# One ring of weight tiles over three phases, and an FFN down projection taken by blocks of tokens

## The chip, the cores and the metric

The kernel runs on one core of a Trainium2 chip. The metric is the device time of one execution in microseconds (us). Engines are called as the profile calls them: PE (matmuls), PEld (the weight loads that go with them), DVE, ACT and POOL (elementwise work), SP (it issues most DMAs). PE's clock is granted at one of two levels, 2.4 GHz (1.00 in the profile) or 1.2 GHz (0.50).

## The reference, cut to what matters

512 tokens of width 1024 pass through two blocks. The first has a projection into attention, a state-space branch and gates, a cross attention over 256 memory tokens, and PEER, a layer of 16384 single-neuron experts. The second has a mixer of two linear-attention kinds and a convolutional FFN:

```python
h = h + merged @ w_out                       # phase 0
h = h + memory_cross_attention(...)          # phase 0
h = h + peer_ffn(rmsnorm(h), ...)            # phase 1: u = u_tab[e]; v = v_tab[e]
x = rmsnorm(h, norm_final)
x = x + rms_norm(hybrid_mixer(rms_norm(x)), norm_mix_post)                        # phase 2
x = x + rms_norm(conv_ffn(rms_norm(x)), norm_ffn_post)                            # phase 2
def conv_ffn(hn):
    g = dwconv3(hn @ w_gate)                 # 1024 -> 2816 = 22 tiles of 128
    return (gelu(g) * (hn @ w_up)) @ w_down  # 2816 -> 1024
```

## The kernel before

**Weights.** Every product is made from three matmuls: each operand is split into a high part and a low remainder, and high x high, high x low and low x high are added in PSUM. `wtile` (L161) does this for a weight tile of 128 x 1024: SP loads `raw` (L170), ACT writes `whi` (L172), DVE or POOL subtracts to get `wlo` (L175). Each of the three has a ring of buffers. The rings belong to a pool `wp` that `phase` (L1751) opens anew in each of three phases: 3, 2 and 2 buffers in phases 0 and 2, and 5, 4 and 4 in phase 1 (`WB`). A new pool lies on memory that the phase before has used, so its tiles wait until the last reader of that memory is done.

**Order.** The order on each engine is fixed when the program is built, from the order of the code and an estimate of when operands are there. An engine doesn't overtake at run time.

**Phase 0** ends with the output projection of the cross attention (8 weight tiles `w_co`), each of which adds into `h` (L872). **Phase 1**, `peer`: `peer_query` splits the normed activations (`fsh` on ACT, L245, `fsl` on DVE, L246), squares them for the norm (L263, L267) and runs 16 projections with `w_pq`. Then come 64 steps of `dense_u` (L1051, UONLY = 64), the U stage: the 384 tokens of three blocks against 128 experts each, 24 matmuls of 384 columns, and a gelu on ACT (L1057) into `al`, which four steps share and which is spilled to DRAM (`ad`, L1059), 768 KB at a time. Among these steps `peer_route` finds the experts, `gate_chunk` (L994) builds 12 chunks of dense gates, ACT copying them (L1014) into the staging tiles `stg` (two buffers of the tag, two tiles per chunk) and SP writing them out (L1017), and from step 32 on 24 gathers for the first token block: POOL's indirect DMAs into the ring `gr` of six buffers (L1022) and a DVE product (L1034). The V stage then runs 64 more `dense_u` and 128 `dense_v` with the spilled values read back.

**Phase 2** begins with `block2` (L1213): splits `bh`, `bl`; one projection (B2P = 1), `rms_pair` (L1180: 16 squares, sums on DVE and POOL at L1193, 16 matmuls at L1196 that sum over partitions, a chain of small steps that gives `rt`), `rbcast` (`rB`), then `proj_small` (48 columns for gates and low-rank inputs), three more projections, and `gates2` (L1353), a chain over ACT and DVE that gives `la` and `cum`. Four projections with a convolution follow (`mqk`, L1269 on), and a stepwise interleaving of `gla`, `mlstm` and three token-major projections `tm(0)` to `tm(2)`, whose matmuls fill PE between the others' steps. Four PSUM banks have the tag "mm", four "sm".

**FFN** (L1708): for three groups of `m` (8, 8 and 6 tiles of the 22), the gate and up projections of each `m`, its convolution, gelu and product, then the down projection of that group: for each of the 8 output tiles, 24 (18) matmuls with a weight tile of `w_fd` standing in PE and 512 tokens moving. Sums go to `ff` in SBUF, feature-major like the residual `x` (in `hx`). After the last tile the norm runs over the features, which lie on partitions: squares, sums, `rms_end` (L270), `rbcast` (L282), and `postnorm` (L1666) with two elementwise operations per tile of 128 x 512 on DVE and POOL, and eight output DMAs.

## Time and profile before

| | us |
|---|---|
| median of 3 runs (2997.66 to 2999.61) | 2999.13 |
| the profiled execution, its own time | 2997.53 |
| its span, first to last instruction | 2995.4 |
| PE busy | 2854.2 (95%), 14033 matmuls |
| DVE, ACT, POOL busy | 2138.7, 1276.9, 765.6 |

The profiled execution is 1.6 us below the median. Its span is 2.1 us shorter than its time. The mean granted clock of PE is 0.979. The rows on which the prediction rests stand behind the diff. "Releaser" is the instruction that ended an idle time. The start of an instruction is in us from the start of the span.

### The profile page before, as it was taken

Reading aid. Unit: us, or ns where it says so; the run is one execution under the profiler, and the core shown is the slowest. Engines: PE = TensorE matmul, PEld = TensorE weight load, DVE = VectorE, ACT = ScalarE, POOL = GpSimd, SP = SyncE. Lnnn points to the kernel's source line nnn. Section 1 sums busy time; section 2 is a strip of 40 time slices with the busy share of each in tenths; the row PEclk is TensorE's granted clock in tenths of the full one; section 3 lists DMA queues with packets and bytes.
Section 4 is the critical chain, followed back from the end, with each engine's and each line's share of the span. In section 5 each row is a group of like instructions: output and inputs, shape, how many; then the busy total and the mean of one; then the engine's idle time right before and its main releaser. Section 6 shows DMA issues by size and latency. Waiting matters only on the chain. (4 is left out here: it accounts for less than half of the span.)

```text
span 2995.4 us, 37951 instructions
## 1 busy us (share of the span) xinstructions
PE 2854.2 (95%) x14033; PEld 2415.6 (81%) x14033; DVE 2138.7 (71%) x3766; ACT 1276.9 (43%) x2159; POOL 765.6 (26%) x529
## 2 busy tenths in 40 slices
PE   7899999999998999989999999999988899799997
PEld 6767788888886899889988888888866677688886
DVE  7987865454557999986677777787875765564656
ACT  4356754332534347776333333333334343332222
POOL 3421320001201010111244444444533551310102
PEclk9999999999999999999999999999998899899998
DMA  4211112324412256778799899999932112233332
GB/s 134 78 53 47 64 57 96 100 85 141 141 57 91 93 197 201 232 240 263 271 332 339 327 345 327 339 329 336 345 147 70 57 43 64 63 99 98 98 93 70
DMA packets 177865, 491.36 MB, mean 164 GB/s; under 512 B 14833, under 2 KB 66289, under 8 KB 177489
## 3 DMA queue, kind: packets, MB, share of 16 engines
q1 hardware_dynamic: 140336, 353.42, 34.7%
q0 software_dynamic: 37344, 135.54, 12.9%
q8 instruction: 110, 1.80, 0.2%
q14 instruction: 75, 0.61, 0.1%
HBM read 445.84 MB, written 41.94 MB: 163 GB/s over the span
## 5 line engine op out<-in xcount | busy, mean ns | idle before, releaser
L172 ACT ACTIVATE whi<-raw 128x1024 fp32r<-128x1024 f32 (+2 forms) x508 | 535.1, 1055 | 1156.4 <-PE mm L187 446.4
L175 DVE TENSOR_TENSOR wlo<-raw,whi 128x1024 fp32r<-128x1024 f32 (+1 forms) x470 | 606.2, 1292 | 346.1 <-ACT whi L172 340.9
L186 PE MATMUL u<-nsh,whi 128*128 128x384 f32 x1024 | 346.2, 338 | 2.7 <-ACT al L1057 2.7
L1022 POOL DMA_INDIRECT gr<-u_tab,pidx x128 | 184.0, 1437 | 641.1 <-DVE gr L1034 490.8
L188 PE MATMUL u<-nsh,wlo 128*128 128x384 f32 x1024 | 345.0, 337 | 0.2 <-DVE wlo L175 0.2
L187 PE MATMUL u<-nsl,whi 128*128 128x384 f32 x1024 | 344.8, 337 | 0.0
L1022 POOL DMA_INDIRECT gr<-v_tab,pidx x128 | 199.9, 1562 | 214.0 <-DVE acc L1047 182.1
L1087 PE MATMUL acc<-whi,Wh 128*128 128x512 f32 x768 | 237.7, 391 | 0.0
L1089 PE MATMUL acc<-whi,Wl 128*128 128x512 f32 x768 | 237.0, 390 | 0.0
L186 PEld LDWEIGHTS u<-nsh,whi 128*128 128x128 f32 x1024 | 192.6, 188 | 5.3 <-ACT al L1057 3.0
L1093 PE MATMUL acc<-wlo,Wh 128*128 128x512 f32 x768 | 194.9, 389 | 0.0
L187 PEld LDWEIGHTS u<-nsl,whi 128*128 128x128 f32 x1024 | 192.7, 188 | 2.3
L188 PEld LDWEIGHTS u<-nsh,wlo 128*128 128x128 f32 x1024 | 192.3, 188 | 0.5 <-DVE wlo L175 0.5
L186 PE MATMUL mm<-ah,whi 128*128 128x512 f32 x424 | 173.1, 408 | 12.5 <-ACT whi L172 12.5
L188 PE MATMUL mm<-ah,wlo 128*128 128x512 f32 x424 | 170.0, 401 | 1.2 <-DVE wlo L175 1.2
L187 PE MATMUL mm<-al,whi 128*128 128x512 f32 x424 | 170.2, 401 | 0.0
L1089 PEld LDWEIGHTS acc<-whi,Wl 128*128 128x128 f32 x768 | 144.1, 188 | 31.4
L1093 PEld LDWEIGHTS acc<-wlo,Wh 128*128 128x128 f32 x768 | 144.1, 188 | 30.0
L1047 DVE SCALAR_TENSOR_TENSOR acc<-gr,act,acc 128x1024 f32<-128x1024 f32 x127 | 163.4, 1287 | 1.5
L1087 PEld LDWEIGHTS acc<-whi,Wh 128*128 128x128 f32 x768 | 143.3, 188 | 26.3
L1034 DVE SCALAR_TENSOR_TENSOR gr<-gr,xt 128x1024 f32<-128x1024 f32 x128 | 153.1, 1221 | 0.0
L186 PE MATMUL mm<-fh,whi 128*128 128x512 f32 x352 | 138.8, 396 | 7.2 <-ACT fh L245 7.2
(596 smaller groups left out, 6311.1 us busy)
## 6 DMA issues: line engine op xcount, KB each, us to landing
raw<-uT SPq DMA_DIRECT2D x128, 512.0 KB, 5.6
raw<-v_tab SPq DMA_DIRECT2D x128, 512.0 KB, 6.5
raw<-w_cm SPq DMA_DIRECT2D x61, 512.0 KB, 3.5
gd<-stg SPq DMA_DIRECT2D x24, 1024.0 KB, 8.4
Gl<-gd SPq DMA_DIRECT2D x32, 768.0 KB, 8.9
ad<-al SPq DMA_DIRECT2D x16, 768.0 KB, 5.7
al<-ad SPq DMA_DIRECT2D x16, 768.0 KB, 7.8
raw<-w_fg SPq DMA_DIRECT2D x22, 512.0 KB, 3.5
```

What stands on the lines that cost most here:

```text
L172: nc.scalar.activation(hi[:, :n], raw[:, :n], AF.Copy)
L175: self.paced = (eng or nc.vector).tensor_tensor(lo[:, :n], raw[:, :n], hi[:, :n].bitcast(F), op=OP.subtract)
L186: mm(ps, w[0][:, cs[k]], xh, start=k0 + k == ends[0], stop=False)
L187: mm(ps, w[0][:, cs[k]], xl, start=False, stop=False)
L188: mm(ps, w[1][:, cs[k]], xh, start=False, stop=k0 + k == k1)
L1022: self.nc.gpsimd.indirect_dma_start(out=t, out_offset=None, in_=self.I[tab], in_offset=bass.IndirectOffsetOnAxis(ap=self.idx[:, j:j + 1], ...
L1034: nc.vector.scalar_tensor_tensor(u, u, 1.0, self.xt, op0=OP.mult, op1=OP.mult, accum_out=self.act0[:, i:i + 1])
L1047: nc.vector.scalar_tensor_tensor(self.acc0, v, w, self.acc0, op0=OP.mult, op1=OP.add)
L1087: mm(self.accp[tt * 2 + hf], wh[:, ts], hi[:, cs[hf]], start=first, stop=False)
L1089: mm(self.accp[tt * 2 + hf], wl[:, ts], hi[:, cs[hf]], start=False, stop=False)
L1093: mm(self.accp[tt * 2 + hf], wh[:, ts], lo[:, cs[hf]], start=False, stop=last)
```

## The change

- `wp` is opened once, outside the phases, with rings of 3, 2 and 2; phase 1 gets a second pool `wpx` with 2, 2 and 2, and tiles take turns between the two, so the depths in each phase stay as they were.
- `gate_chunk` has four staging buffers in place of two.
- In the U stage the gelu writes into `al2`, a tile of two steps, taken from the ring `gr` that the gathers use, and is spilled in pairs (384 KB).
- `block2` starts with `proj_small` and three projections (B2P = 3) before `rms_pair`; `gates2` moves ahead of the evacuation of the projections; `tm(0)` runs as a whole before the `mqk` loop.
- The down projection turns round: `w_fd` is taken in rows, 22 tiles of 128 x 1024; the activations `gs` stand in PE and the weights move; eight PSUM banks collect 4 token blocks x 2 halves. The last `m` of a group (in the last group the last three, whose weights have slab tiles of their own, `own=True`) runs token block by token block. `x` is turned into token-major `xt` by 32 transposes in the first four `m`, `ff` lies in the memory of `hx`, the gain is a row `gB`, and the norm is a sum along the free axis (`accum_out` of the square). The output is written as rows of tokens, in halves.

```diff
@@ -96 +96 @@
     o["w_fu"] = _cm(a["ffn_w_up_2"][0])
-    o["w_fd"] = _cm(a["ffn_w_down_2"][0])
+    o["w_fd"] = a["ffn_w_down_2"][0]
+    o["frow"] = a["norm_ffn_post_2"]
     g = {
@@ -161 +162 @@
 
-    def wtile(self, src, n, eng=None):
+    def wtile(self, src, n, eng=None, own=False):
         nc = self.nc
...
             eng = nc.gpsimd
-        br, bh, bl = WB[self.ph]
-        raw = self.wp.tile([128, 1024], F, name="raw", tag="raw", bufs=br)
+        pick = lambda n, m: self.wpx if self.ph == 1 and self.wi % m >= n else self.wp
+        raw = pick(3, 5).tile([128, 1024], F, name="raw", tag="raw", bufs=pick(3, 5) is self.wp and 3 or 2)
         nc.sync.dma_start(raw[:, :n], src)
-        hi = self.wp.tile([128, 1024], R, name="whi", tag="whi", bufs=bh)
+        if own:
+            s = self.sl("wown", R)
+            hi, lo = s[:, 0:1024], s[:, 1024:2048]
+            nc.scalar.activation(hi, raw, AF.Copy)
+            nc.vector.tensor_tensor(lo, raw, hi.bitcast(F), op=OP.subtract)
+            return hi, lo
+        hi = pick(2, 4).tile([128, 1024], R, name="whi", tag="whi", bufs=2)
         nc.scalar.activation(hi[:, :n], raw[:, :n], AF.Copy)
-        lo = self.wp.tile([128, 1024], R, name="wlo", tag="wlo", bufs=bl)
+        lo = pick(2, 4).tile([128, 1024], R, name="wlo", tag="wlo", bufs=2)
         self.wi += 1
@@ -228 +235 @@
             mm(ps[0:n, :], lo[:, c], acts(k)[0], start=False, stop=k == 7)
-        return self.small_tm(ps, 0, n)
+        return ps
 
@@ -993 +1000 @@
         nc = self.nc
-        stg = [self.mid.tile([128, 2048], F, name="stg", tag="stg", bufs=2) for i in range(2)]
+        stg = [self.mid.tile([128, 2048], F, name="stg", tag="stg", bufs=4) for i in range(2)]
         for q in range(8):
@@ -1051 +1058 @@
         self.mms(ps[:, :384], (hi, lo), self.ns, 0, 8, 8)
+        if a < UONLY:
+            if a % 2 == 0:
+                self.al2 = self.gp.tile([128, 1024], F, name="al2", tag="gr")[:, 0:768].rearrange("p (a t) -> p a t", a=2)
+            nc.scalar.activation(self.al2[:, a % 2, :], ps[:, :384], AF.Gelu)
+            if a % 2:
+                q = a % 4 // 2 * 768
+                nc.sync.dma_start(self.ad[a // 4][:, q:q + 768], self.al2.rearrange("p a t -> p (a t)"))
+            return
         if a % 4 == 0:
...
         nc.scalar.activation(al[:, a % 4, :], ps[:, :384], AF.Gelu)
-        if a < UONLY and a % 4 == 3:
-            nc.sync.dma_start(self.ad[a // 4], al.rearrange("p a t -> p (a t)"))
 
@@ -1117 +1130 @@
                     self.peer_query()
-                self.mid = open_(c1, "umid", UMB)
+                self.mid = open_(c1, "umid", 1)
                 for i, tt in enumerate(ROUTE):
@@ -1218 +1231 @@
             self.split_scaled(acts(k), h(k), self.gfp[:, k:k + 1])
+        psm = self.proj_small(I["w2_g"][0], acts, 48)
         gps = [self.proj_cm(I["w2_cm"][4 + m], acts) for m in range(B2P)]
+        pv = self.small_tm(psm, 0, 48)
         r1, rt = self.rms_pair(h)
...
         self.rh2 = rh
-        pv = self.proj_small(I["w2_g"][0], acts, 48)
         gqk = self.sl("gqk").rearrange("p (k t) -> p k t", k=4)
+        self.gq, self.gk = (lambda i: gqk[:, i, :]), (lambda i: gqk[:, 2 + i, :])
+        ag = self.ag = self.wk("ag", (128, NT, 48), bufs=1)
+        nc.vector.tensor_tensor(ag, pv[:, :, 0:48], rt[:, :, None].to_broadcast([128, NT, 48]), op=OP.mult)
+        nc.vector.tensor_tensor(ag[:, :, 0:16], ag[:, :, 0:16],
+                                self.gr("mgb")[:, None, :].to_broadcast([128, NT, 16]), op=OP.add)
+        self.gates2()
         for m in range(4):
...
                 nc.vector.tensor_tensor(gqk[:, m, :], ps, rB, op=OP.mult)
-        self.gq, self.gk = (lambda i: gqk[:, i, :]), (lambda i: gqk[:, 2 + i, :])
-        ag = self.ag = self.wk("ag", (128, NT, 48), bufs=1)
-        nc.vector.tensor_tensor(ag, pv[:, :, 0:48], rt[:, :, None].to_broadcast([128, NT, 48]), op=OP.mult)
-        nc.vector.tensor_tensor(ag[:, :, 0:16], ag[:, :, 0:16],
-                                self.gr("mgb")[:, None, :].to_broadcast([128, NT, 16]), op=OP.add)
-        self.gates2()
         self.V1 = V1 = self.wk("V1", (128, NT, 4, 130), bufs=1)
@@ -1262 +1276 @@
                 yield from g
-        tms = chain(tm(0), tm(1), tm(2))
+        for _ in tm(0):
+            pass
+        tms = chain(tm(1), tm(2))
         mqk = self.sl("mqk").rearrange("p (k t) -> p k t", k=4)
@@ -1714 +1730 @@
         rB = self.rbcast(self.rms(x))
-        ff = self.pair("ff")
-        self.postnorm_open()
+        xt = [self.sl(f"xt{i}").rearrange("p (t c) -> p t c", t=2) for i in range(2)]
+        gB = self.sl("gB")
+        nc.sync.dma_start(gB[:, 1024:2048], bass.AP(tensor=I["frow"].tensor, offset=0, ap=[[0, 128], [1, D]]))
+        nc.vector.tensor_scalar(gB[:, 0:1024], gB[:, 1024:2048], 32.0, None, op0=OP.mult)
+        ff = None
         for m0, m1 in ((0, 8), (8, 16), (16, 22)):
@@ -1735 +1754 @@
                 self.split_plain(gs(m - m0), y)
-            for m in range(8):
-                ps = self.proj_cm(I["w_fd"][m][:, m0 * 128:m1 * 128], gs, kcs=m1 - m0)
-                if m0 == 0:
-                    nc.vector.tensor_copy(ff(m), ps)
-                elif m0 == 8:
-                    nc.vector.tensor_tensor(ff(m), ff(m), ps, op=OP.add)
-                else:
-                    self.postnorm_in(m, ps, ff(m), "fpost2", ff(m))
-
-        def then(k):
-            nc.sync.dma_start(self.O["out_0_dram"][:, k, :], x(k))
-        self.postnorm(ff, x, "out", then)
+                if m < 4:
+                    for hf in range(2):
+                        pt = self.ps("sm")
+                        for k in range(4):
+                            self.transpose(pt[:, k * 128:(k + 1) * 128], x(hf * 4 + k)[:, m * 128:(m + 1) * 128])
+                        nc.scalar.activation(xt[m // 2][:, m % 2, hf * 512:(hf + 1) * 512], pt, AF.Copy)
+            if ff is None:
+                hf2 = [self.hp.tile([128, 2, 1024], F, name=f"ff{i}", tag=f"hx{i}") for i in range(2)]
+                ff = lambda tt, hf: hf2[tt // 2][:, tt % 2, hf * 512:(hf + 1) * 512]
+            acc = {(tt, hf): self.ps("mm" if tt < 2 else "sm") for tt in range(NT) for hf in range(2)}
+            mm = nc.tensor.matmul
+            cs = [slice(hf * 512, (hf + 1) * 512) for hf in range(2)]
+            n1 = m1 - 3 if m1 == 22 else m1
+            ws = {}
+            for m in range(m0, m1):
+                ws[m] = self.wtile(I["w_fd"][m * 128:(m + 1) * 128, :], 1024, own=m >= n1)
+
+                def main(tt, m=m):
+                    hi, (gh, gl) = ws[m][0], gs(m - m0)
+                    ts = slice(tt * 128, (tt + 1) * 128)
+                    for hf in range(2):
+                        mm(acc[tt, hf], gh[:, ts], hi[:, cs[hf]], start=m == m0, stop=False)
+                    for hf in range(2):
+                        mm(acc[tt, hf], gl[:, ts], hi[:, cs[hf]], start=False, stop=False)
+
+                def rest(tt, m=m):
+                    lo, gh = ws[m][1], gs(m - m0)[0]
+                    for hf in range(2):
+                        mm(acc[tt, hf], gh[:, tt * 128:(tt + 1) * 128], lo[:, cs[hf]], start=False, stop=m == m1 - 1)
+                if m < min(n1, m1 - 1):
+                    for f in (main, rest):
+                        for tt in range(NT):
+                            f(tt)
+            for tt in range(NT):
+                for m in range(min(n1, m1 - 1), m1):
+                    main(tt, m)
+                    rest(tt, m)
+            if m1 < 22:
+                for (tt, hf), ps in acc.items():
+                    if m0:
+                        nc.vector.tensor_tensor(ff(tt, hf), ff(tt, hf), ps, op=OP.add)
+                    elif hf:
+                        nc.vector.tensor_copy(ff(tt, hf), ps)
+                    else:
+                        nc.scalar.activation(ff(tt, hf), ps, AF.Copy)
+        ss = self.wk("fss", (128, NT, 4), bufs=1)
+        for tt in range(NT):
+            t = []
+            for hf in range(2):
+                f = ff(tt, hf)
+                nc.vector.tensor_tensor(f, f, acc[tt, hf], op=OP.add)
+                sq = self.wk("sq")
+                nc.scalar.activation(sq, f, AF.Square, accum_out=ss[:, tt, hf:hf + 1])
+                t.append(self.wk("fo"))
+                nc.vector.tensor_tensor(t[hf], f, gB[:, cs[hf]], op=OP.mult)
+            nc.vector.scalar_tensor_tensor(ss[:, tt, 2:3], ss[:, tt, 0:1], EPS * 1024, ss[:, tt, 1:2],
+                                           op0=OP.add, op1=OP.add)
+            nc.gpsimd.tensor_tensor(ss[:, tt, 3:4], ss[:, tt, 2:3], self.mhalf[:, 0:1], op=OP.pow)
+            for hf in range(2):
+                nc.vector.scalar_tensor_tensor(t[hf], t[hf], ss[:, tt, 3:4], xt[tt // 2][:, tt % 2, cs[hf]],
+                                               op0=OP.mult, op1=OP.add)
+                nc.sync.dma_start(self.O["out_0_dram"][tt * 128:(tt + 1) * 128, cs[hf]], t[hf])
 
@@ -1755 +1824 @@
                 tc.tile_pool(name=f"{name}{n}", bufs=bufs, reuse_waits="tile", **kw))
-            self.wp = pool("wp", 1)
+            if n == 1:
+                self.wpx = pool("wpx", 1)
             if own:
@@ -1773 +1843 @@
             self.const = ctx.enter_context(tc.tile_pool(name="const", bufs=1))
-            hp = ctx.enter_context(tc.tile_pool(name="hp", bufs=1))
-            hx = [hp.tile([128, 4, 512], F, name=f"hx{i}") for i in range(2)]
+            hp = self.hp = ctx.enter_context(tc.tile_pool(name="hp", bufs=1))
+            hx = [hp.tile([128, 4, 512], F, name=f"hx{i}", tag=f"hx{i}") for i in range(2)]
             self.hx = hx
...
             self.xdram = dr.tile([8, 128, 512], F, name="xd")
+            self.wp = ctx.enter_context(tc.tile_pool(name="wp", bufs=1))
             self.setup()
@@ -1794 +1865 @@
 
-WB = ((3, 2, 2), (5, 4, 4), (3, 2, 2))
-GB, PTMP, UMB, VMB = 6, 6, 2, 11
+GB, PTMP, VMB = 6, 6, 11
 QN = 2
@@ -1812 +1882 @@
 GA = (3,)
-B2P = 1
+B2P = 3
 X2P = False
@@ -1843 +1913 @@
          for n, v in a.items()}
-    O = {"out_0_dram": nc.dram_tensor("out_0_dram", [128, 8, T], F, kind="ExternalOutput").ap()}
+    O = {"out_0_dram": nc.dram_tensor("out_0_dram", [T, D], F, kind="ExternalOutput").ap()}
     with tile.TileContext(nc) as tc:
...
     y = r.results[0]["out_0_dram"]
-    return np.ascontiguousarray(y.transpose(2, 1, 0)).reshape(1, T, D)
+    return np.ascontiguousarray(y).reshape(1, T, D)
```

## Rows read from the trace of the kernel before

**Rows 1.** Page, part 1: busy time, share of the span, instructions of PE.
```profile
PE 2854.2 (95%) x14033; PEld 2415.6 (81%) x14033; DVE 2138.7 (71%) x3766; ACT 1276.9 (43%) x2159; POOL 765.6 (26%) x529
```
**Rows 2.** Waits of PE, whole span: total us, times, longest.
```profile
PE mm L186 <- ACT whi L172: 24.7, 4, 11.8
...
PE mm L1343 <- DVE xp L1273: 7.0, 1, 7.0
...
PE sm L1196 <- DVE sa L1193: 5.6, 1, 5.6
...
PE mm L1012 <- ACT stg L1014: 3.2, 4, 1.4
```
**Rows 3.** Busy by stage: stretch, length, PE, PEld, DVE, ACT, POOL, clock, DMA.
```profile
914.00:925.40 11.40, 0.00 (x0) 0.00 (x0) 11.19 (x22) 6.08 (x11) 5.74 (x8) 0.69 0.41 150
...
1045.00:1455.00 410.00, 388.32 (x2421) 376.20 (x2420) 343.72 (x853) 264.71 (x534) 38.55 (x31) 0.99 0.67 221
1455.00:2222.00 767.00, 767.00 (x3697) 674.90 (x3696) 597.10 (x580) 262.61 (x276) 347.16 (x227) 1.00 0.90 327
2222.00:2260.00 38.00, 27.43 (x120) 18.56 (x119) 29.05 (x46) 20.09 (x33) 14.97 (x12) 0.82 0.13 42
2260.00:2320.00 60.00, 52.32 (x221) 39.97 (x220) 36.16 (x53) 27.41 (x28) 18.02 (x8) 0.92 0.21 70
...
2625.00:2972.00 347.00, 346.61 (x1529) 286.44 (x1527) 204.87 (x266) 99.83 (x116) 33.20 (x25) 1.00 0.29 90
2972.00:2995.40 23.40, 4.30 (x26) 3.79 (x24) 14.53 (x14) 1.23 (x2) 11.04 (x7) 0.60 0.24 90
```
**Rows 4.** Timeline of ACT, 908 to 928: start, us, line, out<-in, idle before.
```profile
923.79 0.63 ACT L263 ACTIVATE sq<-hx 128x512 f32<-128x512 f32 x1 [4.18 <-DVE sa L267]
924.33 3.88 ACT L172 ACTIVATE whi<-raw 128x1024 fp32r<-128x1024 f32 x4
```
**Rows 5.** Chain that ended last, 2536 to 2542: start, us, what.
```profile
2538.95 0.23 PE mm L188
2539.19 0.98 PE sm L294 x9
```
**Rows 6.** Timeline of DVE, 908 to 928.
```profile
914.71 0.98 DVE L246 SCALAR_TENSOR_TENSOR fsl<-hx,gcols,fsh 128x512 fp32r<-128x512 f32 x1
...
916.42 6.74 DVE L246 SCALAR_TENSOR_TENSOR fsl<-hx,gcols,fsh 128x512 fp32r<-128x512 f32 x7
```
**Rows 7.** Timeline of PE, 2240 to 2256: the head of block2.
```profile
2246.48 3.58 PE L1196 MATMUL sm<-ones,sa 128*128 128x1 f32 x16 [5.65 <-DVE sa L1193]
...
2250.36 0.63 PE L227 MATMUL mm<-bl,whi 128*48 128x512 f32 x1
2250.78 0.63 PE L226 MATMUL mm<-bh,whi 128*48 128x512 f32 x1
```
**Rows 8.** Waits of ACT in the U stage, 1045 to 1455.
```profile
ACT stg L1014 <- DMA gd<-stg: 3.4, 2, 1.7
```
**Rows 9.** DMA issues: count, KB each, median us from issue to landing.
```profile
ad<-al SPq DMA_DIRECT2D x16, 768.0 KB, 5.7
...
gr<-u_tab,pidx POOLq DMA_INDIRECT x128, 7.5
```
**Rows 10.** Timeline of DVE, 2224 to 2232: the start of phase 2.
```profile
2228.32 2.10 DVE L175 TENSOR_TENSOR wlo<-raw,whi 128x1024 fp32r<-128x1024 f32 x1
```
**Rows 11.** Chain that ended last, 2965 to the end.
```profile
2972.43 0.70 DVE ff L1653
2973.15 0.64 ACT sq L1659
...
2975.89 1.03 POOL rstd L280
...
2991.63 0.69 DVE hx L1671
```
**Rows 12.** Groups by form, 2184 on: busy us, mean ns, idle before.
```profile
L1731 DVE SCALAR_TENSOR_TENSOR cy<-xp,gcols,cy 128x512 f32<-128x512 f32 x44 | 33.0, 749 | 0.8
```

## The prediction

> **What bounds the kernel now.** I read the busy times first: PE is busy for 2854 of 2995 us [rows 1], so the change can win at most the other 141 us, plus what PE loses at its lower clock. The number of projection matmuls stays the same, so gains must come from places where PE waits or runs at 1.2 GHz. The waits of PE name them [rows 2]: 24.7 us for a weight's high part in four places (one of 11.8), 7.0 for DVE's evacuation `xp`, 5.6 for the sums of `rms_pair`, 3.2 for the staging tile. The table by stage places them [rows 3]: nothing from 914 to 925.4 (the start of phase 1); 21.7 of 410 us idle in the U stage; none in the 767 us of the V stage; 10.6 of 38 and 7.7 of 60 at the start of phase 2; 0.4 of 347 in the FFN; and 19 of 23.4 behind its last product. V stage and FFN body are filled by PE: there the change can only add. I take the other places one by one.
>
> **Start of phase 1.** PE waits until 925.4 for `whi`. Its copy stands on ACT behind the eight squares, whose last waited 4.18 us for a sum [rows 4]. Its memory belonged to phase 0's pool, so the copy could not be placed earlier. With one ring its slot is free one weight tile before phase 0 ends, some 24 x 0.23 = 5.5 us [rows 5]. Then the first projection needs only `fsl`, which DVE makes from 914.7 to 923.2 [rows 6], and ends near 923.7 instead of starting at 925.4. The second weight's slot is freed by the last tile of phase 0, and its copy can still lie behind the squares, so the second projection starts where the first starts now. The gain is one projection: 5.5 us at 2.4 GHz, 24 x 0.42 = 10 at 1.2 (the step between two matmuls at that level [rows 7]); the clock is mixed here (0.69 [rows 3]), so I take **7.5**. Ends: 0 if the copy stays behind the squares, 11.8 if the whole wait goes. What is late next is `fsl` on DVE.
>
> **U stage.** Staging: ACT waited twice for a staging tile to be written out, 3.4 us in all [rows 8], and PE 3.2 us for ACT's copies [rows 2]. Four buffers make that wait go: **-3**. The spill in pairs moves `al2` into the gathers' ring and issues 32 DMAs where 16 were. Queued behind the new waits are: on ACT, the gelu, with the next `whi` behind it; on POOL, the next gather, and for its landing DVE's product, with `wlo` behind it; on SP, 16 more issues ahead of `raw` loads. A pair holds a buffer for two steps of 410/64 = 6.4 us and a landing of at most 5.7 (of twice the size [rows 9]): 18.5 us. Per two steps the ring gives out one pair and, with a gather every 1.3 steps, 1.5 gathers, so six buffers turn in 6/2.5 x 12.8 = 31 us. That covers it, and covers a gather's 7.5 [rows 9] too, so I cost it at nothing; if the cover goes, see the last rival. Other orders on ACT and DVE, which are loaded here (344 of 410 us on DVE [rows 3]), can move the stage by some us: -8 to +3 for the whole part.
>
> **Start of phase 2.** DVE did the first `wlo` (2.10 us) between the updates of `h` for which the first projection waits [rows 10]. With one ring that remainder can be made before the V stage's last matmuls are done: -1.5 (0 to -2.1). Then `rms_pair`: PE waits 5.65 us for the sums, having only one projection to do meanwhile, and runs the next 24 matmuls at the lower clock [rows 7]: 16 small ones at 0.22 instead of about half, and eight full ones at 0.42 instead of 0.23, 1.8 + 1.6 = 3.4. Now `proj_small` and three projections stand ahead, 96 x 0.23 = 22 us from about 2230 to 2252, and the sums are there at 2246.5. So 5.65 + 3.4 go. What comes late next: `rt` is made by a chain of small steps behind the sums, all four "mm" banks are full until `rB` exists, and PE does one more projection, 5.5 us, meanwhile; I add back 1. Sum for the head: 1.5 + 5.65 + 3.4 - 1 = **-9.5**.
>
> Further on, PE waits 7.0 us for `xp`, which stands on DVE behind the `gates2` chain [rows 2]. That chain now starts ahead of the `mqk` projections, and `tm(0)` gives PE 96 matmuls, 22 us, that need nothing from it. Against it, those 22 us are no longer there to fill the steps of `gla` and `mlstm`. I take half of the 7.0: **-3.5**. Ends for the whole of `block2`, head included: -3 (the rest is given back later) and -25 (what PE lacks in the first two stretches of rows 3, 18 us, and their lower clock).
>
> **FFN.** Body: the count of matmuls in the down projection is the same, 22 x 24. In the V stage, where activations stand and weights move, and in the FFN, where it is the other way round, PE is filled alike [rows 3], so the turn costs nothing. Added are 32 transposes: nine took 0.98 us, 0.109 each [rows 5], 3.5 us on PE. At each group's start the eighth bank waits for the last evacuation, 0.7 us on DVE, against 1.1 us in which PE uses other banks, and at its end the banks are freed block by block: +1 for all (0 to 3). ACT's eight copies and the row `gB` lie beside PE's work (100 of 347 us busy on ACT [rows 3]).
>
> The TensorE page of the Trainium skill (TensorE: Matmul & The Clock Gate, "Part 4: PE-mode transpose") speaks against the transposes: about 275 ns each in one kernel's context, as an estimate 32 x 0.275 = 8.8 us, with which the FFN would gain 5 us less. The trace doesn't agree, at 0.109 us each among matmuls of this kernel; I go by that row.
>
> Tail: from the last product at 2972.43 to the end at 2995.4 are 23.0 us, a chain through sums, `rstd`, the broadcast and two elementwise operations per tile [rows 11]. Now only the last token block is left behind its last matmul: two additions at 0.70, two products with the gain at 0.70 (one of them in the square's shadow), a square at 0.64, the power at 1.03, two final operations at 0.75 [rows 11, 12], and, as an estimate, 0.8 for the small sum and the steps between: 0.70 x 3 + 0.64 + 1.03 + 1.5 + 0.8 = 6.1. Then the last write: 3.1 us, as from the end of the last `hx` to the end of the span [rows 11]. That is 9.2, and as DVE needs about as long for a block (4.5 us) as PE for its 18 matmuls (4.1), 0.3 for the block before: 9.5. The tail gives -13.5 (ends -12 and -14.5). FFN in all: 3.5 + 1 - 13.5 = **-9**, from -6 to -11.
>
> **Sum.** -7.5 - 3 - 13 - 9 = -32.5, on the profiled execution's own 2997.5: 2965. The median is 1.6 above it, so I forecast **2966**; the case's own range, with the ends of its terms, is 2950 to 2980.
>
> **Rivals.** (1) The one ring doesn't do what it says: the first copy of phase 1 stays behind the squares on ACT. For it: the order on an engine is fixed, and the squares come first in the code. Against it: their operands come later than the weight. Then 7.5 is lost: 2974. (2) The gain in `block2` is given back: with `tm(0)` gone from the fillers, PE waits for the steps of `gla` and `mlstm`. For it: PE already waits there with `tm(0)` among them. Against it: the chain that these need starts earlier as well. Then 13 less 3 is lost: 2976; with (1), 2984. (3) Slower: the shared ring `gr` delays the gathers, and DVE, in order, waits for landings ahead of `wlo`. At its worst 24 gathers cost the full 7.5 each, 180 us. DVE has 410 - 344 = 66 us to spare [rows 3], so it decides from 66/24 = 2.8 us per gather, and to end above the time before it must eat up 33 us of gain, at 4.1 each. At the full price: 344 + 180 - 410 = 114 us more, 3080. Against it stands the turn of 31 us against 18.5.
>
> **How the numbers follow.** My forecast 0.68; (1) alone 0.10; (2) alone 0.12; both 0.05; (3) 0.05. For the range of 8 in 10 I add the outer ends: more than forecast in `block2` and the U stage (12 and 5 us, both rarely) down to 2946, and (1) with (2) up to 2988. A measurement of this kernel tells about 0.2%, 6 us, from no change: faster means below 2993. My forecast and (1), (2) are faster but for a tenth of bad luck in the order of ACT and DVE, which is shared between the same and slower: faster 0.87, same 0.06, slower 0.07.
>
> **What the profile after would show.** Right: the first matmul with `fsh` before 916, and PE's idle time there under 4 us; no wait for `stg` on ACT; L1196's counterpart without idle time ahead of it, and no stretch at 1.2 GHz around it; the V stage at 767 us; the FFN's body some 4 us longer; less than 11 us from the last matmul to the end. Wrong: `whi` still behind the squares, DVE waiting for gathers between 1250 and 1455, PE's idle time between `block2`'s `mqk` projections and the end of the mixer above what it is now, or weights missing at the groups' borders in the FFN.

## The result and the profile after

The changed kernel takes 2963.74 us (median, 2961.28 to 2964.78), the kernel before beside it 2998.68: a ratio of 0.988, 95% interval 0.9865 to 0.990. The forecast was 2966. The profiled execution took 2963.61 us and its span is 2961.5. The first part of the page after, as in [rows 1]:

```profile
PE 2846.9 (96%) x14041; PEld 2412.5 (81%) x14041; DVE 2133.2 (72%) x3759; ACT 1282.8 (43%) x2176; POOL 756.7 (26%) x523
```

The same table by stage as [rows 3], with the borders where the changed kernel has them (stretch, length, PE, PEld, DVE, ACT, POOL, clock, DMA share, GB/s):

```profile
914.40:916.30 1.90, 0.39 (x2) 0.00 (x0) 1.47 (x5) 1.70 (x3) 1.43 (x6) 1.00 0.77 196
1028.20:1441.30 413.10, 396.76 (x2490) 387.20 (x2489) 354.41 (x894) 272.27 (x541) 42.94 (x32) 0.99 0.69 223
1441.30:2204.30 763.00, 763.00 (x3673) 670.80 (x3672) 595.26 (x581) 261.98 (x276) 347.05 (x226) 1.00 0.90 329
2204.30:2234.70 30.40, 27.96 (x134) 19.96 (x133) 25.30 (x34) 19.94 (x31) 12.06 (x9) 1.00 0.12 35
2234.70:2311.00 76.30, 61.57 (x271) 48.53 (x272) 38.01 (x74) 30.16 (x31) 30.02 (x17) 0.84 0.16 49
...
2558.60:2576.90 18.30, 6.41 (x29) 5.14 (x28) 11.78 (x11) 5.92 (x9) 10.03 (x7) 0.57 0.17 58
2576.90:2951.80 374.90, 371.06 (x1637) 306.74 (x1638) 220.56 (x281) 114.96 (x147) 42.08 (x33) 0.98 0.28 89
2951.80:2961.50 9.70, 0.42 (x2) 0.00 (x0) 5.30 (x9) 1.33 (x4) 0.82 (x2) 0.78 0.29 108
```

And PE's waits over the whole span, against [rows 2] (total us, times, longest):

```profile
PE mm L193 <- ACT whi L179: 14.3, 4, 12.2
...
PE mm L193 <- ACT fh L252: 7.2, 1, 7.2
...
PE sm L1494 <- DVE me L1602: 3.6, 1, 3.6
...
PE sm L1501 <- POOL EQ L1482: 3.2, 1, 3.2
```

The wait for `whi` at the start of phase 1 is gone (what is left is the very first matmul of the kernel, 12.2), and so are those for `xp` (7.0) and for the sums (5.6 then, 0.7 now). New is the 3.6 in the steps of `gla`. The wait of PE for `EQ` from POOL isn't new; in the kernel before it is

```profile
PE sm L1485 <- POOL EQ L1466: 5.6, 2, 4.9
```

New as well, and each too short to stand among the longest of the whole span, are waits in the first 70 us of `block2` behind the gates chain, of 1.0 to 2.8 us each, which an expectation below lists.

For the account I took the first or last PE instruction of each stage in both traces, so that the differences add up. PE's first matmul of a tile marks a border: `fsh` (phase 1), `u`, `acc` (V stage), `bh` (`block2`), `y2` (its last projection), `fh` (FFN).

| stretch | before | after | difference | predicted |
|---|---|---|---|---|
| up to the last matmul of phase 0 | 913.27 | 914.40 | +1.1 | 0 |
| to the first `u` | 124.57 | 113.82 | -10.8 | -7.5 |
| U stage, to the first `acc` | 421.73 | 413.12 | -8.6 | -3 |
| V stage, to the last `acc` | 763.00 | 763.01 | 0 | 0 |
| to the first `bh` | 8.60 | 6.46 | -2.1 | -1.5 |
| `block2`, to the last `y2` | 350.5 | 347.8 | -2.7 | -11.5 |
| to the first `fh` | 15.7 | 15.7 | 0 | 0 |
| FFN, to its last product | 374.6 | 377.5 | +2.9 | +4.5 |
| from there to the end | 23.4 | 9.7 | -13.7 | -13.5 |
| sum | 2995.4 | 2961.5 | -33.9 | -32.5 |

That the sum came out is luck: two misses went in opposite directions. `block2` gave 9 us less than I counted, the U stage and the start of phase 1 together 9 more. The experiments are about these three, and about the last three weights of the FFN. Phase 0 is untouched, and its end lies between 913.1 and 917.0 in the fourteen profiled kernels of this study; that is how much of a difference of single executions means nothing.

### The profile page after: what moved, and what is told of

Its sections match the earlier page's. It is cut to its first block, busy times and chain, and to the rows that moved or that the text cites. A ratio compares the mean times of both kernels' runs of the same rounds, so it can differ in the third digit from the quotient of the medians.

```text
span 2961.5 us, 38029 instructions
## 1 busy us (share of the span) xinstructions
PE 2846.9 (96%) x14041; PEld 2412.5 (81%) x14041; DVE 2133.2 (72%) x3759; ACT 1282.8 (43%) x2176; POOL 756.7 (26%) x523
## 4 chain that ended last, share of the span: by engine, by line
PE 78%; DVE 11%; ACT 5%; issue 2%; POOL 1%; DMA 0%; DVEq 0%; POOLq 0%; ACTq 0%; SPq 0%
PE mm L195 9%; PE mm L194 9%; PE mm L193 9%; PE acc L1100 6%; PE acc L1102 6%; PE acc L1106 6%; PE u L194 5%; PE u L193 5%; PE u L195 5%; ACT stg L1021 2%; PE mm L1361 2%; PE mm L1362 2%; PE mm L1359 2%; PE sm L301 1%; PE mm L1019 1%
## 5 line engine op out<-in xcount | busy, mean ns | idle before, releaser
L179 ACT ACTIVATE whi<-raw 128x1024 fp32r<-128x1024 f32 x503 | 532.3, 1059 | 1127.4 <-PE mm L194 366.2
L182 DVE TENSOR_TENSOR wlo<-raw,whi 128x1024 fp32r<-128x1024 f32 x465 | 605.4, 1305 | 390.6 <-ACT whi L179 327.8
```

The source lines that it names most:

```text
L179: nc.scalar.activation(hi[:, :n], raw[:, :n], AF.Copy)
L182: self.paced = (eng or nc.vector).tensor_tensor(lo[:, :n], raw[:, :n], hi[:, :n].bitcast(F), op=OP.subtract)
```

## The experiments

**The ring of the weights: pools per phase again.**

```diff
...
-            if n == 1:
-                self.wpx = pool("wpx", 1)
+            self.wp = pool("wp", 1)
...
+WB = ((3, 2, 2), (5, 4, 4), (3, 2, 2))
```

> Undoes the one ring alone: the weight pool is opened anew in each phase, as before the change, with everything else of the changed kernel kept. Theory: the ring is what brought the start of phase 1 forward by 9.6 us (10.8 without the 1.1 us by which phase 0 ends later) and the border of phases 1 and 2 by 2.2; so the first fsh matmul goes back from 916 to about 925, and the time is 2964 + 13 = 2977. Rival: ACT does the copies early because its order around the squares differs by the other edits, and the memory alone costs little: first fsh before 919, time 2964 to 2968. A third possibility is that a later start is caught up in the U stage, whose waits are on DVE: the first acc matmul then comes less than 5 us later than in the changed kernel.

Measured: 2975.75 us, ratio 0.992 (0.991 to 0.994). The first `fsh` matmul is at 927.1, 12.2 us behind the end of phase 0, where the changed kernel has 1.9. ACT's timeline with pools per phase (start, us, line, operation, idle time before):

```profile
925.48 0.63 ACT L270 ACTIVATE sq<-hx 128x512 f32<-128x512 f32 x1 [4.18 <-DVE sa L274]
926.01 3.88 ACT L179 ACTIVATE whi<-raw 128x1024 fp32r<-128x1024 f32 x4
```

and in the changed kernel:

```profile
909.16 1.06 ACT L179 ACTIVATE whi<-raw 128x1024 fp32r<-128x1024 f32 x1 [4.38 <-PE mm L194]
910.77 2.01 ACT L179 ACTIVATE whi<-raw 128x1024 fp32r<-128x1024 f32 x2 [0.55 <-DMA raw<-w_pq]
914.60 1.06 ACT L179 ACTIVATE whi<-raw 128x1024 fp32r<-128x1024 f32 x1 [1.82 <-PE mm L194]
```

With pools per phase the four copies stand behind the last square and its wait of 4.18 us, as in [rows 4]; with one ring three of them are done before phase 0 ends, and the fourth follows at 914.60, ahead of the squares too. So the ring alone brings 10.2 us. At the border of phases 1 and 2 it brings 1.1 of the 2.1 us (7.6 with pools per phase, 6.5 with the ring). The U stage, however, is 411.2 us in this kernel: its gain has nothing to do with the ring of the weights. `block2` took 352.5 us here, 4.7 more than in the changed kernel, at a lower clock; this is told of at the end.

**Two staging tiles.**

```diff
-        stg = [... tag="stg", bufs=4) for i in range(2)]
+        stg = [... tag="stg", bufs=2) for i in range(2)]
```

> Two staging tiles in place of four, everything else of the changed kernel kept. The U stage became 8.6 us shorter where the prediction had 3. Theory A: all of the 8.6 comes from the staging tiles, since ACT, which waits for a staging tile, also holds up the weight copies behind it: U stage from 413 back to about 421, time 2972. Theory B: the staging tiles are worth the 3.2 us that PE waited at L1012 and no more, the other 5 come from an order on DVE and ACT that changed with the pairs in al2 and with the earlier start: U stage about 416, time 2967.

Measured: 2965.54 us, 0.989 (0.9875 to 0.991); U stage 414.0. Theory A falls: the stage is 1 us longer, not 8.6. ACT's wait for a written-out tile comes back (3.1 us).

But 1 us is too little for the staging tiles, as PE's clock wasn't the same. Nine of the profiled kernels have the changed kernel's U stage, with the same instructions in the same order. In six of them PE ran 3.4 us of it at 1.2 GHz, and it lasted 411.2 to 411.7 us; in three, the changed kernel among them, 6.8 us, and it lasted 413.1 to 413.3. Here is one such stretch, in the changed kernel (0.51, 14 matmuls), and the same place of the stage with pools per phase (1.00, 28 matmuls):

```profile
1329.00:1332.40 3.40, 3.40 (x14) 3.40 (x13) 3.40 (x11) 1.82 (x5) 1.40 (x1) 0.51 1.02 380
1341.00:1344.40 3.40, 3.40 (x28) 3.40 (x27) 3.40 (x12) 2.82 (x7) 1.40 (x1) 1.00 1.02 401
```

With two staging tiles it was 3.4 us. So against the six the staging tiles are worth 2.4 to 2.9 us, and a difference of 2 us between two U stages can be the clock.

**The spill in fours again, with two staging tiles.**

```diff
...
-            nc.scalar.activation(self.al2[:, a % 2, :], ps[:, :384], AF.Gelu)
-            if a % 2:
...
-                nc.sync.dma_start(self.ad[a // 4][:, q:q + 768], ...)
...
         nc.scalar.activation(al[:, a % 4, :], ps[:, :384], AF.Gelu)
+        if a < UONLY and a % 4 == 3:
+            nc.sync.dma_start(self.ad[a // 4], al.rearrange("p a t -> p (a t)"))
...
-                self.mid = open_(c1, "umid", 1)
+                self.mid = open_(c1, "umid", 2)
```

> Undoes the spill in pairs on top of two staging tiles: the gelu writes into tiles of four in the U stage's own pool (two buffers, one DMA of 768 KB each) as before the change. Two staging tiles with pairs gave a U stage of 414.0 us and 2965.5 in all; the kernel before has 421.7. Theory: the pairs are the rest of the stage's gain (ACT's gelu no longer waits for a tile of four to be written out, and the copies for the gates behind it on ACT come on time): U stage 420 to 422, time 2972 to 2974. Rival: the pairs change nothing, and the stage is shorter because it starts at another point against the gathers and gate chunks: U stage 413 to 416, time 2964 to 2967.

Measured: 2977.19 us, 0.9925 (0.991 to 0.994); U stage 422.5. The stage has the instructions of the kernel before again, in their order, and that one's length (421.7). So the pairs, which I had costed at nothing, carry 8.4 us; some of it is the clock, since PE ran 10.2 us of this stage at 1.2 GHz (6.8 in the kernel before) against 3.4 with pairs. The time is above the theory's 2972 to 2974, because `block2` took 352.4 us in this kernel; that is told of at the end. The pairs can act by the size of the transfer or by their place in the gathers' ring; the next two runs ask which.

**Pairs in a pool of their own** (with two staging tiles, like the two runs before).

```diff
-                self.al2 = self.gp.tile([128, 1024], F, name="al2", tag="gr")[:, 0:768]...
+                self.al2 = self.mid.tile([128, 768], F, name="al2", tag="al2", bufs=4)...
```

> Spill in pairs, with two staging tiles as in the two kernels that it is compared with (pairs in the gathers' ring: U stage 414.0 us; tiles of four in the stage's own pool: 422.5), but the pairs have four buffers of their own in the U stage's pool and take none from the gathers' ring. It tells what the 8.4 us between those two come from. Theory: the size of the spill decides (an issue per two steps, each of half the size, in another place of the queues): U stage 413 to 416. Rival: the place decides (a turn of the gathers' ring paces gathers and gate chunks differently): U stage 420 to 423.

Measured: 2975.18 us, 0.992 (0.991 to 0.994); U stage 424.5, with 13.7 us at 1.2 GHz. The theory falls and the rival holds, 1.5 us beyond its range: pairs of the same size give nothing when they don't take turns with the gathers. What the turns do is seen in DVE's products of the gathers (`gr`, line 1041; each counts twice, with the read of its accumulator), in two stretches: from the first `u` to the 56th weight, and from there to the end of the stage. The rows count 26 products, since the first two of the V stage's own fall into the second stretch. Spill in fours:

```profile
1028.16:1379.50 351.34, 25.71 (x42) 0.99 0.65 215
1379.50:1450.60 71.10, 6.12 (x10) 1.00 0.70 239
```

pairs in a pool of their own:

```profile
1026.94:1380.40 353.46, 25.81 (x42) 0.98 0.66 214
1380.40:1451.50 71.10, 6.13 (x10) 1.00 0.71 235
```

pairs in the gathers' ring:

```profile
1029.97:1373.40 343.43, 21.96 (x36) 1.00 0.66 210
1373.40:1444.00 70.60, 9.81 (x16) 1.00 0.85 285
```

In the first stretch DVE also makes `A` and `B` for the gate matmuls, and PE waits for `A`; in most of the second there are no gates. The pairs hold the ring's buffers. POOL's first gather, with the spill in fours and with pairs in the ring:

```profile
1068.02 4.31 POOL L1029 DMA_INDIRECT gr<-u_tab,pidx  x1 [125.51 <-DVE pidx L993]
1158.93 2.26 POOL L1029 DMA_INDIRECT gr<-u_tab,pidx  x1 [214.62 <-ACT whi L179]
```

These are 40 and 129 us into the stage. In fours six gathers are issued by 51 us, as the ring is empty; in the ring with pairs three by 179. By the 32nd weight DVE has done one product where it had 3, and 18 of 24 lie in the crowded stretch instead of 21. The second stretch takes up the rest at no cost.

**The same delay without the ring.** Spill in fours and two staging tiles, with the edits shown above, but the gathers begin three weights later:

```diff
-SP0, SP1, NSP, VSP = 32, 1.3, 24, 124
+SP0, SP1, NSP, VSP = 35, 1.3, 24, 124
```

> Tiles of four in the stage's own pool and two staging tiles, as in the kernel with a U stage of 422.5 us; only the 24 gathers with their products begin 3 weights later (at the 35th weight in place of the 32nd). Where pairs take turns in the gathers' ring, POOL issues 2 gathers ahead of the first product instead of 6 to 8, and DVE has done 18 of 24 products (1.25 us each) by the 56th weight instead of 21; the rest falls into the stretch without gate chunks, where DVE has time. Theory: these 2 to 3 products, moved out of the stretch in which DVE is late with A and B, are what the pairs give: U stage 414 to 418, time 2968 to 2972. Rival: it is another effect of the ring (the order of SP's queue or of ACT's gelu): U stage 421 to 424, time 2975 to 2977.

Measured: 2971.50 us, 0.991 (0.989 to 0.992); U stage 418.8, with 19 products in the first stretch:

```profile
1028.58:1376.20 347.62, 23.28 (x38) 0.99 0.64 213
1376.20:1447.30 71.10, 8.50 (x14) 1.00 0.74 258
```

Its U stage is between both theories: the later products by themselves give 3.7 of the 8.4 us, or 3.0 against the kernel before, which has the same 6.8 us at 1.2 GHz. The order is the same in all four kernels (21, 21, 19, 18 products; 422.5, 424.5, 418.8, 414.0 us), but that the remaining 4.7 come from the last product isn't shown: some 2 of them can be the clock (6.8 us at 1.2 GHz here, 3.4 with pairs in the ring), and the rest another effect of the ring's turns. The whole stage of the four, and of the changed kernel's order with pools per phase (columns as in [rows 3]; fours, own pool, three weights later, pairs in the ring, pools per phase):

```profile
1028.20:1450.60 422.40, 401.21 (x2490) 389.19 (x2489) 354.01 (x892) 271.84 (x541) 40.60 (x32) 0.99 0.66 219
1026.90:1451.50 424.60, 402.30 (x2491) 390.27 (x2490) 354.63 (x894) 272.04 (x542) 41.18 (x32) 0.98 0.67 217
1028.60:1447.30 418.70, 399.79 (x2490) 387.66 (x2489) 354.67 (x892) 272.40 (x541) 41.54 (x32) 0.99 0.66 221
1030.00:1444.00 414.00, 395.67 (x2490) 385.65 (x2489) 354.24 (x892) 272.67 (x541) 43.56 (x32) 1.00 0.69 223
1040.22:1451.45 411.23, 395.35 (x2491) 385.77 (x2490) 354.13 (x892) 272.44 (x541) 41.78 (x32) 1.00 0.70 225
```

Length less busy time, PE's idle time, is 21.2, 22.3, 18.9, 18.3 and 15.9 us: by this measure the later products alone give most of what the pairs give. Nor is it shown that DVE is what PE is late for: of PE's waits for `A` the trace puts 10.7 us down to the quarter that ACT makes and 2.8 to DVE's (spill in fours), 9.2 and 1.1 with pairs in the ring.

**The order of `block2` as before.**

```diff
-        psm = self.proj_small(I["w2_g"][0], acts, 48)
         gps = [self.proj_cm(I["w2_cm"][4 + m], acts) for m in range(B2P)]
-        pv = self.small_tm(psm, 0, 48)
...
+        pv = self.small_tm(self.proj_small(I["w2_g"][0], acts, 48), 0, 48)
...
+        for m in range(4):
+            ps = gps[m] if m < B2P else self.proj_cm(I["w2_cm"][4 + m], acts)
...
         self.gates2()
-        for m in range(4):
-            ps = gps[m] if m < B2P else self.proj_cm(I["w2_cm"][4 + m], acts)
...
-        for _ in tm(0):
-            pass
-        tms = chain(tm(1), tm(2))
+        tms = chain(tm(0), tm(1), tm(2))
...
-B2P = 3
+B2P = 1
```

> Undoes all edits in the order of block2 and keeps the rest: one projection ahead of the sums, proj_small and the gates chain back behind the evacuation of gqk, tm(0) back among the fillers. Theory: what the head gained there was given back further on, so block2 from its first bh matmul to its last y2 was shortened by 2.7 us only; the wait of 5.6 us for the sums and that for xp (7.0) come back, those in mlstm_prep go, and the time is 2966 to 2967. Rival: these edits are worth the 11 to 13 us that the prediction gave them, and something else in the changed kernel (the shared ring for the weights, which now carries phase 1's sizes into phase 2) costs block2 some 9 us: time about 2975.

Measured: 2960.97 us, 0.9875 (0.986 to 0.989), no slower than the changed kernel and 5 us below the theory's time; `block2` 346.5 us. Neither theory has the time. The border ahead of `block2` is 7.4 us instead of 6.5: the other 1.0 of its 2.1 us comes from the order. All of the edits in `block2` together are worth nothing that can be measured. The wait for `xp` is back, with 7.0, and that for the sums with 3.0; PE's waits in `gla` for POOL are 7.7 instead of 3.2, and of those in `mlstm_prep` only 1.6 is left.

**`tm(0)` among the fillers.**

```diff
-        for _ in tm(0):
-            pass
-        tms = chain(tm(1), tm(2))
+        tms = chain(tm(0), tm(1), tm(2))
```

> Puts tm(0), 96 projection matmuls of 22 us, back among the fillers of gla and mlstm; the early gates and the three projections ahead of the sums stay. Theory: tm(0) done at once is what PE lacks later; with it as filler the waits in mlstm (L1494 3.6, L1501 3.2) shrink, but those in mlstm_prep (L1549, L1560, L1562, 6 us) and for gqk become longer, since the gates chain then has 22 us less of cover: time within 3 us of 2964. Rival 1: the filler alone decides, block2 becomes 6 to 10 us shorter, 2955 to 2958. Rival 2: the cover alone decides, block2 becomes 6 to 10 us longer, 2970 to 2974.

Measured: 2961.60 us, 0.987 (0.9855 to 0.989); `block2` 347.9. Neither rival decides.

**The gates chain behind the evacuation of `gqk`.**

```diff
-        self.gates2()
         for m in range(4):
             ps = gps[m] if m < B2P else self.proj_cm(I["w2_cm"][4 + m], acts)
...
+        self.gates2()
```

> Moves the gates chain alone back behind the evacuation of gqk; proj_small and three projections stay ahead of the sums, tm(0) stays at once. In the changed kernel gqk is evacuated at 65 to 68 us after the first bh matmul, because DVE does the gates chain first, and the four banks that it holds are what keeps PE from tm(0) while the chain and mlstm_prep run (waits of 1.04, 1.62, 2.83, 1.59, 1.70 us). Theory: with gqk evacuated at about 33 to 36 us PE does tm(0) beside the chain, these waits shrink by 5 us or more, but mlstm and gla begin later and end at the same place: block2 345 to 348 us, time 2961 to 2964. Rival: PE's idle time there is saved for good: block2 340 to 343, time 2956 to 2959. Third: as in the kernel before, xp behind the chain makes PE wait 7 us: block2 350 or more, time 2966.

Measured: 2963.36 us, 0.988 (0.987 to 0.990); `block2` 346.2. `gqk` is evacuated at 33 to 38 us after the first `bh` matmul instead of 65 to 68, PE's idle time between 25 and 75 us falls from 12.2 to 3.9, as the theory has it, and then PE waits once for 8.5 us, for a `wlo` on POOL. The gain doesn't last.

**Fillers given out more slowly.**

```diff
-GLAP, TMP2, MLP = (1, 1, 1), (0, 2, 3), (0, 1, 1)
+GLAP, TMP2, MLP = (1, 1, 1), (0, 1, 2), (0, 1, 1)
```

> The fillers of gla and mlstm are given out more slowly: one piece in two steps instead of two pieces in three, so that the ten pieces that are left (tm(1) and tm(2), without tm(0)) last for 20 of the 22 steps instead of 15. In the changed kernel PE's idle time in block2 is 19.6 us in the first 150 us and 9.1 in the next 150; in the kernel before it is 25.2 and 3.0. Theory: the late idle time is there because the fillers run out, so it falls to 4 to 6 us and block2 is 343 to 345 us long, time 2959 to 2961. Rival: the sum of idle time stays at about 30 us wherever the fillers lie, since each piece that is moved is missing where it was: block2 346 to 349, time 2962 to 2965.

Measured: 2967.47 us, 0.9895 (0.988 to 0.991); `block2` 350.7. Both were wrong: the idle time rose to 38.1 us, 7.6 more, of which 2.9 are left in the length of the block. 9.0 of it is one wait in `gla`, for `EQ` from POOL (PE's waits from 2205 to 2562):

```profile
PE sm L1501 <- POOL EQ L1482: 10.2, 2, 9.0
PE sm L1501 <- DVE me L1602: 3.4, 2, 2.1
```

From 2450 to 2475 us, around this wait, PE began no projection matmul, in the changed kernel 28. So my reading that the late waits stand where the ten pieces have run out is not right as it stands. It may be that PE comes to the next work (`tm(3)`) sooner when the pieces are given out sooner, and that stretching them delays that; no run shows it.

`block2` of these kernels side by side, in two lines each: 150 us from the first `bh` matmul, and the rest up to the last `y2` (columns as in [rows 3]). The kernel before:

```profile
2231.20:2381.20 150.00, 124.83 (x516) 91.73 (x517) 102.64 (x188) 63.76 (x96) 67.00 (x42) 0.87 0.19 67
2381.20:2581.70 200.50, 195.64 (x952) 154.79 (x952) 122.24 (x264) 82.17 (x185) 70.63 (x61) 0.97 0.20 61
```

the changed kernel:

```profile
2210.80:2360.80 150.00, 130.37 (x542) 98.11 (x543) 98.59 (x157) 66.23 (x88) 68.53 (x44) 0.90 0.21 67
2360.80:2558.60 197.80, 186.93 (x925) 146.07 (x924) 134.10 (x292) 80.68 (x196) 71.55 (x61) 0.97 0.18 56
```

the changed kernel with the gates chain late:

```profile
2211.00:2361.00 150.00, 131.20 (x551) 98.23 (x552) 103.13 (x157) 67.51 (x89) 73.32 (x42) 0.90 0.21 67
2361.00:2557.20 196.20, 183.93 (x915) 142.75 (x914) 135.48 (x292) 79.25 (x194) 74.64 (x63) 0.98 0.18 57
```

the changed kernel with the spill in fours, whose `block2` has the order of the changed one:

```profile
2220.10:2370.10 150.00, 132.27 (x521) 97.67 (x522) 99.41 (x157) 63.46 (x85) 64.94 (x41) 0.84 0.21 67
2370.10:2572.50 202.40, 191.52 (x946) 149.86 (x945) 135.05 (x293) 83.33 (x199) 76.26 (x64) 0.97 0.18 55
```

Length less busy time is PE's idle time. Before: 25.2 and 4.9. After: 19.6 and 10.9. With the gates late: 18.8 and 12.3. In the order of before, within the changed kernel, it is 23.1 and 7.2, and with `tm(0)` as filler 23.6 and 7.6. In these five what the head gains the rest of the block loses, and the sum stays between 30.0 and 31.2 us. The last pair of rows shows a second thing: less idle time (28.6 us) and yet 4.6 us longer, at a lower clock in the first 150 us (0.84 against 0.90).

**Only the last weight token block by token block.**

```diff
-            n1 = m1 - 3 if m1 == 22 else m1
+            n1 = m1
```

> The last three weights of the down projection are no longer kept: only the last one runs token block by token block. The sums of the first token blocks then all become ready within 6 matmuls (1.4 us) of each other, where 18 matmuls (4.1 us) lie between them in the changed kernel, and DVE needs about 4.5 us for each block. Theory: after the last matmul DVE has some 2.5 blocks to do instead of one: the tail is 9.7 + 3 x (4.5 - 1.4) less the slack of 0.4 each, some 17 to 19 us, time 2971 to 2973. Rival: the blocks overlap on ACT, POOL and DVE, and the tail grows by less than 4 us: time 2964 to 2968.

Measured: 2969.41 us, 0.991 (0.989 to 0.992). From the last product to the end it takes 17.1 us:

```profile
2949.40:2966.50 17.10, 0.36 (x2) 0.00 (x0) 11.95 (x22) 3.44 (x11) 2.40 (x3) 0.63 0.33 123
```

DVE has 22 operations, 11.95 us, left there, where the changed kernel has 9 and 5.30 (last line of the table by stage). The theory's tail of 17 to 19 holds; its time was 2 us too high, as the stages ahead of the tail are 2.5 us shorter in this execution. Of the 13.7 us that the tail gained, 6.3 come from the turned product and its sums by token (23.4 to 17.1) and 7.4 from the three kept weights.

**Not part of the change: the normalisation ahead of the FFN on DVE alone.**

```diff
-PNP = (5, 6, 7)
+PNP = ()
```

> Not part of the change: POOL's share of the normalisation between the mixer and the FFN (three of eight tiles) goes to DVE. In the changed kernel PE waits 7.2 us there for fh and runs 20.5 us at the lower clock behind it; DVE's operations last 1.7 us each while POOL works on its share, against 0.69 alone. Theory: DVE alone is sooner done, as its operations last 0.69 us each: 8 x 0.69 = 5.5 us for a pass against 5 x 1.7 = 8.5, the wait for fh falls by 2 to 5 us, time 2958 to 2962. Rival: DVE then does 8 tiles where it did 5, and the wait stays or grows: time 2963 to 2967.

Measured: 2957.84 us, 0.9865 (0.985 to 0.988), the lowest time of all kernels here; as the interval overlaps that of the changed kernel, its verdict rests on the stage. DVE's groups between the mixer and the FFN in the changed kernel (busy us, mean ns):

```profile
L1686 DVE TENSOR_TENSOR mix<-mix,rB 128x512 f32<-128x512 f32 x3 | 4.1, 1399 | 3.9 <-ACT rB L297 3.9
L253 DVE SCALAR_TENSOR_TENSOR fl<-hx,gcols,fh 128x512 fp32r<-128x512 f32 x2 | 3.4, 1754 | 0.0
L1687 DVE TENSOR_TENSOR hx<-mix,hx 128x512 f32<-128x512 f32 x2 | 3.4, 1744 | 0.0
```

and with POOL out of it:

```profile
L1686 DVE TENSOR_TENSOR mix<-mix,rB 128x512 f32<-128x512 f32 x5 | 3.3, 685 | 3.9 <-ACT rB L297 3.9
L1687 DVE TENSOR_TENSOR hx<-mix,hx 128x512 f32<-128x512 f32 x4 | 2.7, 683 | 0.0
...
L253 DVE SCALAR_TENSOR_TENSOR fl<-hx,gcols,fh 128x512 fp32r<-128x512 f32 x3 | 2.1, 744 | 0.0
```

POOL's share in the changed kernel:

```profile
L1687 POOL TENSOR_TENSOR hx<-mix,hx 128x512 f32<-128x512 f32 x3 | 5.0, 1670 | 0.1
```

The same operation lasts 683 ns on DVE alone and 1744 beside POOL's, which last as long (1670). From the last `y2` to the first `fh` it is 11.0 us instead of 15.7, and the FFN behind it is 3.3 us shorter, since PE runs 7.2 us at the lower clock there instead of 14.2: together 8.0 us, of which `block2`, 3.4 us longer in this execution, takes some back. The Trainium skill has a rule for this (SBUF — State Buffer, "Who interferes with whom"): a DVE instruction with two inputs in SBUF contends with a GpSimd instruction that reads SBUF, and the port pair that they share is an exclusive lock. The rows agree with it: `hx` has two such inputs, and its time is more than doubled.

**Three edits together:** DVE alone, the gates chain late, the fillers slower.

> Not part of the change: three edits together, to see whether a version beats the changed kernel: the normalisation between mixer and FFN on DVE alone (2957.8 us by itself), the gates chain behind the evacuation of gqk (2963.4 by itself) and the fillers given out more slowly. If each edit keeps what it gives by itself: 2963.7 - 5.9 - 0.4 - 3 = 2954 to 2957. If block2's idle time stays at 30 us whatever the order: 2957 to 2960.

Measured: 2959.51 us, 0.987 (0.985 to 0.988). `block2` has the idle time of the slower fillers (37.9 us). It doesn't beat DVE alone.

## Why the prediction came out

**Start of phase 1.** The mechanism was right, the term of 7.5 too small at 10.8. The step that failed is that only the first weight's copy would come ahead of the squares: all four did, three of them before phase 0 ended, so nearly the whole wait of 11.8 went. The two copies at 910.77 waited for the load of their weights and for no buffer. As I read the code, they lie in `wpx`, the second pool, whose buffers no weight of phase 0 holds; the working counted the first pool alone. Rival (1) didn't come true, and pools per phase show what it would have looked like.

**U stage.** The staging tiles, to which I gave the -3, are worth 2.4 to 2.9 us where the clock is the same; that term was right. The step that failed is the pairs, which I costed at nothing because six buffers turn fast enough: they give the larger part, 6 us of the 8.6 as an estimate (8.6 less the 2.4 to 2.9; PE ran 6.8 us of the stage at 1.2 GHz before and after). The working on the ring asked only whether a gather could come too late for DVE (rival 3). It took the gathers to begin at the 32nd weight; with the ring to themselves the first six were issued 40 to 51 us into the stage. The ring did hold them back, and with them DVE's products, and products that are later by three weights gave 3 to 4 us without the ring. That this is the whole gain isn't shown. 344 of 410 us busy [rows 3] told me that DVE had 66 us to spare, but this is a mean: with the spill in fours DVE was busy for 320 of the first 351 us and for 34 of the last 71.

**Start of phase 2 and `block2`.** The border gave 2.1 for 1.5, 1.1 of it from the ring and 1.0 from the order. The wait for the sums fell from 5.65 to 0.72, and that for `xp` went, both as forecast. But what rival (2), at 0.12, says of `block2` is what happened: the gain was given back, and PE's idle time behind the first 150 us rose from 4.9 to 10.9. Its reason, that `tm(0)` is gone from the fillers, isn't borne out alone: with `tm(0)` back among them the late idle time is 7.6, but the early one 23.6, and the block as long. Two steps failed. Behind the sums I added back 1 us, as if the four banks were free with `rB`; their evacuation stood on DVE behind the whole gates chain, and PE had 24 projection matmuls to do between 25 and 50 us, where it had 88. And I counted the gain at a wait as a gain at the end: with the evacuation early again (33 to 38 us) the block took 346.2 us, where the changed order itself took 346.4 with only the last weight in token blocks. Four orders, besides that of the kernel before, were tried; three of them leave the sum of idle time at 30 to 31 us, and the slower fillers raise it. The measured -2.7 is itself no gain of these edits: PE's idle time was 0.5 us longer than before, its busy time 3.1 us shorter, with 41.0 us at 1.2 GHz instead of 51.2, and kernels with the same order in `block2` took 346.4 to 352.6 us there.

What holds the sum at 30 us isn't shown. Starting the chains earlier didn't lower it, and a slower rate of fillers raised it.

**FFN.** The transposes, for which I had 3.5 us, took 3.9: 21 of the 32 stepped at 0.109 us as in [rows 5], seven at 0.213, at the lower clock at the FFN's start, and four, the last of each group of eight, at less. The +1 for the borders of the groups wasn't there: PE's idle time in the body is 5.2 us, before 5.6. The body grew by 2.9 us; what took off the rest isn't shown. Beside this row the prediction weighed 0.275 us for one, from the Trainium skill (TensorE: Matmul & The Clock Gate, "Part 4: PE-mode transpose"). One transpose does last that long here (median 0.272 us, its end modelled), but the next one begins 0.109 us after it. What 32 of them cost goes by the step, and the row was the better guide.

**Tail.** 9.7 for 9.5, and here too two terms missed in opposite directions. The chain of the last token block, on DVE and on POOL for the power:

```profile
2953.44 1.28 DVE L1807 TENSOR_TENSOR ff<-ff,sm 128x512 f32<-128x512 f32 x2
2956.07 0.54 POOL L1814 TENSOR_TENSOR fss<-fss,mhalf 128x1 f32<-128x1 f32 x1 [4.00 <-DVE fss L1812]
2956.65 1.41 DVE L1816 SCALAR_TENSOR_TENSOR fo<-fo,fss,xt 128x512 f32<-128x512 f32 x2 [0.66 <-POOL fss L1814]
```

It took 4.6 us, to 2958.06, where I had 6.1: the power took 0.54 for 1.03, and the square lay in the shadow of DVE's other operations. But DVE came to it 1.6 us after the last product began, where I had 0.3, as it was busy with the block before until then. The write took 3.4 us for 3.1.

## What to carry to other kernels

When an edit removes a wait of the engine that bounds the kernel, sum that engine's idle time over the whole block before and after; here it stayed the same in four orders of the same work. An engine with 16% to spare on the mean can be loaded for 91% in a part of the stage, and work that is not urgent (here products of gathers) is worth trying behind that part. A gain in the tail has nothing behind it that could take it back: work that waits for a last sum should be split so that only one block's share is left behind the last matmul. And a stage that differs by 2 us between two kernels has to be compared at the same time at the lower clock.

## What was not expected of the hardware

In eight of the profiled kernels, the changed one among them, `block2` has the same instructions in the same order on PE (1466), ACT and POOL, and but for one kernel on DVE. It took 346.4 to 352.6 us. In the changed kernel PE ran 41.0 us of it at 1.2 GHz, with only the last weight in token blocks 37.5, with the spill in fours and with pools per phase 58.0. Length less idle time is 317.3, 316.0, 323.8 and 323.9 us: from the second to the third 7.8 us more for 20.5 us at the lower clock, 0.38 for each; the idle time is 1.8 us less, so the block is 6.0 us longer. What went before the block was the same but for the time at which it began (2210.8, 2211.0, 2220.1 and 2222.0 us) and the stages ahead of the V stage. So a difference of some 5 us in a block with many short waits can come from the clock alone, and such a block has to be compared by its idle time and by its clock, each for itself.
